# A two-layer hybrid decoder trunk: order pins at the delta rule's inverse and norm, and two kinds of subtraction and addition moved to GpSimd

## The chip, the cores and the metric

The kernel runs on one core of one Trainium2 chip, in one launch. The metric is the device time of that launch in microseconds (us), taken as the median of several runs. The core has a matrix engine (TensorE, PE in the profile, with its weight loads shown as PEld), three engines that work on elements (VectorE or DVE, ScalarE or ACT, GpSimd or POOL) and queues that start data transfers (here those of SyncE, SP). Each engine takes its instructions in the order in which they stand in its own queue; semaphores order the engines among each other.

## The reference

Two layers, 1024 positions, width 1024, all in float32. Each layer normalises its input, projects it once, and gives slices of the projection to three mixers whose gated outputs go through one output projection and are added to the input. Cut to what matters:

```python
h = rmsnorm(x, norm_gain)
proj = h @ w_in
(gq, gk, gv, gb, ga, gz, mq, mkv, mkr, mz, lx, lz) = split(proj)
# A: gated delta rule, 4 heads of 128, chunks of 64 positions
q, k, v = silu(conv4(gq, gk, gv)); q, k = l2norm(q), l2norm(k)
sol = triangular_solve(tril(k*b @ k.T * decay) + I, [v*b, k*b*exp(g)])
state = state * exp(g_last) + k_n.T @ (u_n - w_n @ state)      # over the chunks
o_a = rmsnorm(o, gdn_out_norm) * silu(gz)
# B: attention with low-rank q and k/v, 8 heads, causal softmax
o_b = attention(q, k, v) * silu(mz)
# C: gated linear recurrence (RG-LRU) over 512 channels
u = conv4(lx) + bias; r, i = sigmoid(u @ w_r + b_r), sigmoid(u @ w_i + b_i)
a = exp(-8 r softplus(-L)); h_t = a_t h_(t-1) + sqrt(1 - a_t**2) i_t u_t
o_c = h * silu(lz)
out = x + concat(o_a, o_b, o_c) @ w_out
```

A last rmsnorm follows the second layer.

## The kernel before

A float32 product is made of three matmuls on split operands (high times high, high times low, low times high; `mm3`, whose records in the profile stand on L132, L133 and L134). A high part is a cast (`whi`, `uh`, `oh`), a low part a subtraction (`wlo`, `ul`, `ol`). `split` does the cast on ScalarE and the subtraction on VectorE unless an engine is given.

Each layer has two phases. **Phase A** runs input tiles (`in_tile`), each 128 output channels by 1024 positions: 48 matmuls into an accumulator `pbig`, of which there are two buffers. Its order in the program is that of `phase_a`: for heads 0, 1 (pr=0) and then heads 2, 3 (pr=1) it calls the steps of the delta rule, and between them `go(k)` draws k steps from a generator of *filler* work: input tiles of other mixers, with the convolutions or gates that belong to them. `gdn_pre` builds the chunk matrices, `gdn_inverse` inverts them on VectorE and sends them through DRAM, `gdn_prep` multiplies with the inverse (first matmul on L442, for q = 0 to 3), `gdn_scan` carries the state over the chunks, `gdn_norm` squares the outputs on ScalarE, makes the factor `ms`, scales `at` with it on GpSimd (L105, 16 scalings of 128x128), transposes it on PE (L525, four groups of four) and gates it on VectorE (`gzh`). After pr=1 comes `lru`: for m = 0 to 3 an input tile LX, its convolution `u` (one ScalarE operation, then three VectorE steps over 1023, 1022 and 1021 columns, L99), the split into `uh` and `ul`, the gate matmuls into `pssc`, and later the recurrence; then four tiles LZ that gate it, and the output projection of the delta rule's and the LRU's blocks.

**Phase C** is attention: per head scores (`pS`, L777 to L781), maxima on VectorE (L787 to L792), exponentials on ScalarE, scaling by the reciprocal sum, transposes (L827), and the product with V (L838 to L840). `out_proj_last` is the last block of the output projection: it splits eight weight tiles (`wl`) into high and low parts, adds the result to the residual, and squares and sums the new residual (`add_squares`, L190) for the next norm.

What runs next on an engine is not the program's order. A scheduler (the tile framework's) lists the instructions by dependencies, its own time estimates and a priority that the program can shift: the input tiles' matmuls are put far back (`prio(LOW)`), so that they fill the gaps, and low parts, gates and convolutions far ahead (`prio(-LOW)`). `keep_in_program_order(i)` ties an instruction behind the instruction of the same engine that was written just before it, without a semaphore. The kernel uses it once, in `gate_sums`. Buffers come from rotating pools, so an instruction may also wait for an older reader of its buffer.

Of the kernel before, what the change touches and what calls it, by code (L numbers as in the profile page):

```python
# [63 lines left out]
class Trunk:  # L64
# [357 lines left out]
    def gdn_prep(self, pr, P, q):  # L422

        nc, pa, con = self.nc, self.pa, self.con
        qs = slice(q * H2, (q + 1) * H2)
        M = pa.tile([128, H2], F32, name="mt", tag="am", bufs=2)
        nc.sync.dma_start(M, self.dn[pr][:, qs])
        TT = pa.tile([128, H2], F32, name="tq", tag="tmat", bufs=1)
        nc.sync.dma_start(TT, self.dz[pr][:, qs])
        bv = pa.tile([128, H2], F32, name="bv", tag="bv", bufs=1)  # L430
        bk = pa.tile([128, H2], F32, name="bk", tag="bk", bufs=1)
        kd = [pa.tile([128, H2], F32, name="kd", tag="kd", bufs=4) for _ in range(2)]
        for c, u, hd, cs in self.combos(q):
            j = q * 4 + c
            gj = u * 4 + 2 * pr + hd
            self.gts(bv[:, cs], P["vtok"][q][:, cs], P["br"][:, j : j + 1])
            self.gts(bk[:, cs], P["ktok"][q][:, cs], P["br2e"][:, j : j + 1])
            for par in range(2):
                self.gts(kd[par][:, cs], P["ktok"][q][:, cs], self.dec[:, par, gj : gj + 1])
        pz = self.bank("pr")  # L440
        for c, u, hd, cs in self.combos(q):
            nc.tensor.matmul(pz[:, cs], M[:, cs], TT[:, cs], start=True, stop=True)  # L442
        z = pa.tile([128, H2], F32, name="z", tag="w1", bufs=1)
        q4 = lambda ap: ap.rearrange("p (c j) -> p c j", c=4)
        self.tt(q4(z), q4(pz), con[:, K_MZ : K_MZ + 128].unsqueeze(1).to_broadcast([128, 4, 128]), ALU.mult)
        py = self.bank("pr")
        for c, u, hd, cs in self.combos(q):
            nc.tensor.matmul(py[:, cs], M[:, cs], z[:, cs], start=True, stop=True)
        tf = pa.tile([128, H2], F32, name="tf", tag="w2", bufs=1)
        self.tt(tf, py, TT, ALU.add)  # L450
        pw = self.bank("pr")
        for c, u, hd, cs in self.combos(q):
            nc.tensor.matmul(pw[:, cs], bk[:, cs], tf[:, cs], start=True, stop=True)
        for hd in range(2):

            base = P["wq"][hd][:, 2 * q : 2 * q + 2, 0:64]
            dst = bass.AP(base.tensor, base.offset, [list(base.ap[0]), list(base.ap[1]), [192, 2], [1, 64]])
            nc.scalar.copy(dst, pw.rearrange("p (u h c j) -> p u h c j", u=2, h=2, c=2)[:, :, hd])
        pu = self.bank("pr")
        for c, u, hd, cs in self.combos(q):  # L460
            nc.tensor.matmul(pu[:, cs], tf[:, cs], bv[:, cs], start=True, stop=True)
        uu = pa.tile([128, H2], F32, name="uu", tag="uu", bufs=2)
        nc.scalar.copy(uu, pu)
        P["u"][q], P["kd"][q] = uu, kd
# [41 lines left out]
    def gdn_norm(self, pr, P):  # L506

        nc, pa = self.nc, self.pa
        jk = pa.tile([128, 128], F32, name="junk", tag="junk", bufs=1)
        ms = pa.tile([128, 16], F32, name="ms", tag="ms", bufs=2)  # L510
        for q in range(4):
            for c, u, hd, cs in self.combos(q):
                last = self.act(jk, P["attn"][q][:, cs], AF.Square, accum_out=ms[:, 4 * q + c : 4 * q + c + 1])
        self.tt(ms, ms, P["rq2"], ALU.mult)
        self.behind(self.act(ms, ms, AF.Ln, scale=1.0 / 128.0, bias=self.eps), self.ln_exp_set(last))
        self.act(ms, ms, AF.Exp, scale=-0.5)
        self.tt(ms, ms, P["rq"], ALU.mult)
        for q in range(4):
            o = P["attn"][q]
            for c, u, hd, cs in self.combos(q):  # L520
                self.gts(o[:, cs], o[:, cs], ms[:, 4 * q + c : 4 * q + c + 1])
            pt = self.bank("pr")
            for c, u, hd, cs in self.combos(q):
                j = hd * 256 + (c // 2) * 128
                nc.tensor.transpose(pt[:, j : j + 128], o[:, cs], self.ident)  # L525
            gz = pa.tile([128, H2], F32, name="gzh", tag="gzh", bufs=2)
            for hd in range(2):
                nc.sync.dma_start(gz[:, hd * 256 : hd * 256 + 256], self.gzd[2 * pr + hd][:, q * 256 : q * 256 + 256])
            self.stt(gz, pt, self.onh, gz, ALU.mult, ALU.mult)
            for hd in range(2):  # L530
                nc.sync.dma_start(self.oad[2 * pr + hd][:, q * 256 : q * 256 + 256], gz[:, hd * 256 : hd * 256 + 256])
# [336 lines left out]
    def out_proj_last(self, wsrc, ops, xin, xout, alloc):  # L868

        nc = self.nc  # L870
        W = []
        for m in range(8):
            if m < 4 or m % 2 == 0:
                w = self.pp.tile([128, 2 if m < 4 else 4, 256], F32R, name="wl", tag="P2" if m < 4 else "P4", bufs=4)
            hi, lo = (w[:, j] for j in ((0, 1) if m < 4 else (2 * (m % 2), 2 * (m % 2) + 1)))
            st = self.pw.tile([128, self.wn], F32, name="wst", tag="wst")
            nc.sync.dma_start(st[:, :256], wsrc[m].rearrange("p k c -> p (k c)"))
            with self.prio(-self.LOW):
                self.split(hi, lo, st[:, :256])
            W.append(tuple(a.rearrange("p (k c) -> p k c", k=2) for a in (hi, lo)))  # L880
        for n in range(2):
            xs, accs = [], []
            for m in range(8):
                if m < 6:
                    xt = self.pc.tile([128, H2], F32, name="xk", tag=("q", "qr")[n], bufs=6)
                elif m == 6:
                    both = self.pc.tile([128, 2, H2], F32, name="xk", tag="ob", bufs=6)
                    xt = both[:, 0]
                else:
                    xt = both[:, 1]  # L890
                self.out_tile(*W[m], ops, n, "pj", xt, xin[m], xout and xout[m])
                with self.prio(-self.LOW):
                    if m % 2 == 0 or m == 7:
                        accs.append(None)
                    accs[-1] = self.add_squares(alloc, accs[-1], xt, (nc.vector, nc.gpsimd)[n])
                xs.append(xt)
            yield n, xs, accs

# [77 lines left out]
    def phase_a(self, l):  # L976
# [31 lines left out]
        def fill0():  # L1008
            yield from gz[0]
            yield from itertools.islice(mz, 8 - self.MZ1 - self.MZ2)  # L1010
            P[1] = self.gdn_new()
            yield from qkv(1, P[1])

        def fill1():
            yield from self.lat_kv(l)
            yield from self.lat_q(l)
            yield from gz[1]
            yield from mz

        for pr, fill, n in ((0, fill0(), self.FILL[0]), (1, fill1(), self.FILL[1])):  # L1020
            def go(k):
                for _ in range(k):
                    next(fill, None)
            Q = P[pr]
            self.gdn_tok(pr, Q)
            go(n[0])
            for q in range(4):
                self.gdn_pre(pr, Q, q)
                go(n[1])
            self.gdn_inverse(pr)  # L1030
            go(n[2])
            self.gdn_prep(pr, Q, 0)
            go(n[3])
            for q in range(4):
                if q < 3:
                    self.gdn_prep(pr, Q, q + 1)
                self.gdn_scan(pr, Q, q)
                go(n[4])
            self.gdn_norm(pr, Q)
            go(99)  # L1040

    MZ1 = 4
    MZ2 = 0
# [177 lines left out]
```

## Time and profile before

| | us |
|---|---|
| median of 3 runs | 2149.24 (2148.1 to 2151.57) |
| the profiled execution | 2147.64 |
| its span, first to last instruction | 2145.7 |
| mean granted TensorE clock | 0.992 of full |

The profile is of one execution. A row of its timeline gives the start in us from the span's begin, the duration in us, engine, line, operation, output and inputs, and shape; xN stands for N such instructions in a row, and a bracket gives the idle time of the engine just before and what ended it. Names drop their buffer numbers. Where the seconds go by engine: PE is busy nearly all the time; VectorE 1302.2, ScalarE 858.0 and GpSimd 719.8 us of the span.

### The profile page before, as it was taken

The page shows a single profiled execution, that of the slowest core. Times are in us where ns is not written, and L with a number is a line of the kernel's source. Part 1 is how long each engine was busy: PE and PEld are TensorE (multiplying, and loading weights), DVE is VectorE, ACT ScalarE, POOL GpSimd, SP SyncE. Part 2 cuts the span into 40 slices and gives each one's busy share as a digit, 9 for nine tenths or more (in the row PEclk, how much of TensorE's full clock was granted, in tenths as well). Part 3 has the DMA queues.
Part 4 walks back from the last instruction along what each step waited for, and adds up shares of the span by engine and source line. Part 5 has one row for each costly group of instructions (what it writes and reads, how often), then busy time and mean ns, then how long its engine had stood idle before and what let it go on. Part 6 is the DMA issues. An engine that isn't in the chain of part 4 may idle for free. (4 is left out here: it accounts for less than half of the span.)

```text
span 2145.7 us, 28793 instructions
## 1 busy us (share of the span) xinstructions
PE 2050.1 (96%) x10380; PEld 1681.6 (78%) x10380; DVE 1302.2 (61%) x2506; ACT 858.0 (40%) x1771; POOL 719.8 (34%) x776
## 2 busy tenths in 40 slices
PE   7999999999989999999899999999998999999997
PEld 4888878787777788888678888787776878888875
DVE  6556546545741777776764575474467237676766
ACT  5241243145620554443542313522375125444534
POOL 2132332333541433332342223333336323332322
PEclk9999999999999999999999999999999999999999
DMA  5123113413254015335511321134223520335163
GB/s 176 55 81 116 55 50 104 124 54 104 69 186 134 23 51 176 115 114 179 188 55 40 113 86 50 64 103 133 69 69 108 181 97 24 111 117 173 56 216 123
DMA packets 135102, 222.07 MB, mean 103 GB/s; under 512 B 37808, under 2 KB 60336, under 8 KB 134960
## 3 DMA queue, kind: packets, MB, share of 16 engines
q1 hardware_dynamic: 134960, 220.24, 31.9%
q8 instruction: 82, 1.34, 0.3%
q14 instruction: 60, 0.49, 0.1%
HBM read 147.31 MB, written 72.88 MB: 103 GB/s over the span
## 5 line engine op out<-in xcount | busy, mean ns | idle before, releaser
L123 POOL TENSOR_TENSOR wlo<-wst,whi 128x1024 fp32r<-128x1024 f32 (+3 forms) x196 | 318.9, 1628 | 849.2 <-DVE whi L122 305.4
L132 PE MATMUL pbig<-h,whi 128*128 128x512 f32 x1216 | 483.9, 398 | 6.7 <-ACT h L138 4.9
L134 PE MATMUL pbig<-h,wlo 128*128 128x512 f32 x1216 | 483.0, 397 | 4.5 <-POOL wlo L123 4.5
L133 PE MATMUL pbig<-h,whi 128*128 128x512 f32 x1216 | 482.4, 397 | 0.1
L132 PEld LDWEIGHTS pbig<-h,whi 128*128 128x128 f32 x1216 | 229.6, 189 | 53.0 <-ACT h L138 6.4
L134 PEld LDWEIGHTS pbig<-h,wlo 128*128 128x128 f32 x1216 | 229.9, 189 | 50.4 <-POOL wlo L123 6.2
L133 PEld LDWEIGHTS pbig<-h,whi 128*128 128x128 f32 x1216 | 229.7, 189 | 44.6 <-issue 1.0
L122 DVE CAST whi<-wst 128x1024 fp32r<-128x1024 f32 x92 | 79.8, 867 | 184.0 <-PE pbig L133 134.2
L86 ACT ACTIVATE P<-pS,mx,scq 128x512 f32<-128x512 f32 (+1 forms) x192 | 128.0, 669 | 155.6 <-DVE mx L790 78.9
L105 POOL TENSOR_SCALAR P<-P,mx 128x128 f32<-128x128 f32 (+6 forms) x112 | 80.4, 719 | 209.4 <-DVE mx L798 119.8
L120 ACT CAST whi<-wst 128x256 fp32r<-128x256 f32 (+2 forms) x104 | 46.6, 448 | 199.6 <-DMA wst<-in_w_uk 96.9
L138 ACT CAST pth<-pstp 128x512 fp32r<-128x512 f32 x192 | 90.6, 478 | 79.1 <-PE pstp L827 77.7
L787 DVE TENSOR_REDUCE mx<-pS 128x1 f32<-128x512 f32 (+1 forms) x192 | 106.6, 555 | 18.1 <-PE pS L781 11.6
L139 DVE TENSOR_TENSOR ptl<-pstp,pth 128x512 fp32r<-128x512 f32 x192 | 104.9, 552 | 15.4 <-ACT pth L138 14.9
L827 PE MATMUL pstp<-con,P 128*128 128x128 f32 x576 | 98.6, 276 | 6.2 <-DVE P L802 5.3
L102 DVE TENSOR_TENSOR xt<-pspj,xt 128x512 f32<-128x512 f32 x96 | 66.3, 690 | 52.5 <-PE pspj L134 24.9
L827 PEld LDWEIGHTS pstp<-con,P 128*128 128x128 f32 x576 | 72.5, 142 | 25.5 <-DVE P L802 7.1
L132 PE MATMUL pspj<-lh,whi 128*128 128x512 f32 x208 | 83.9, 404 | 2.1 <-DVE xt L102 1.8
L838 PE MATMUL pspo<-pth,vh 128*128 128x512 f32 x192 | 79.9, 416 | 4.8 <-ACT pth L138 4.7
L86 ACT ACTIVATE z<-pbig 128x1024 f32<-128x1024 f32 x24 | 24.6, 1026 | 146.2 <-PE pbig L134 143.0
L133 PE MATMUL pspj<-ll,whi 128*128 128x512 f32 x208 | 81.8, 393 | 0.0
L134 PE MATMUL pspj<-lh,wlo 128*128 128x512 f32 x208 | 81.4, 392 | 0.0
(271 smaller groups left out, 4588.6 us busy)
## 6 DMA issues: line engine op xcount, KB each, us to landing
wst<-in_w_in SPq DMA_DIRECT2D x76, 512.0 KB, 3.6
x<-xt SPq DMA_DIRECT2D x128, 256.0 KB, 3.3
xt<-x SPq DMA_DIRECT2D x112, 256.0 KB, 3.3
mzd<-z SPq DMA_DIRECT2D x16, 512.0 KB, 4.5
wst<-in_w_o SPq DMA_DIRECT2D x16, 512.0 KB, 3.5
mz<-mzd SPq DMA_DIRECT2D x32, 256.0 KB, 3.2
wst<-in_w_o SPq DMA_DIRECT2D x64, 128.0 KB, 2.1
xk<-x SPq DMA_DIRECT2D x32, 256.0 KB, 4.6
```

Source lines behind the costliest of these rows:

```text
L86: return self.nc.scalar.activation(out, in_, func, **kw)
L105: self.nc.gpsimd.tensor_scalar(out, a, s, 1.0, ALU.mult, ALU.mult)
L122: nc.vector.tensor_copy(hi[:, :n], st[:, :n])
L123: (eng or nc.gpsimd).tensor_tensor(lo[:, :n], st[:, :n], hi[:, :n].bitcast(F32), ALU.subtract)
L132: nc.tensor.matmul(out, ah, bh, start=(start and j == 0), stop=False)
L133: nc.tensor.matmul(out, ah, bl, start=False, stop=False)
L134: nc.tensor.matmul(out, al, bh, start=False, stop=(stop and j == n - 1))
L138: self.nc.scalar.copy(hi, x)
L139: (eng or self.nc.vector).tensor_tensor(lo, x, hi.bitcast(F32), ALU.subtract)
L787: nc.vector.tensor_reduce(mx[:, j : j + 1], S[j], AX.X, ALU.max, negate=True)
L827: nc.tensor.transpose(tp[:, qi * 128 : qi * 128 + 128], P[qi][:, kb * 128 : kb * 128 + 128], self.ident)
L838: nc.tensor.matmul(po[:, w], vh[:, vs], th[:, w], start=(j == 0), stop=False)
```

## The change

Four edits, each in both layers:

1. In `gdn_prep` the first product on the inverse for q = 0 is tied behind the PE instruction written before it.
2. `gdn_norm` becomes a generator that stops after `ms`. `phase_a` runs it to there, then draws the rest of the filler (`go(99)`), then runs its second half. The first transpose of q = 0 is tied in the same way. So the transposes are written behind all the filler that is left, and pinned there.
3. The last call of `go` for pr = 1 draws one step less.
4. In `out_proj_last` the low parts of the weights, and the sums of squares of the first half of the columns, go from VectorE to GpSimd (8 and 3 per layer).

```diff
@@ gdn_prep
-            nc.tensor.matmul(pz[:, cs], M[:, cs], TT[:, cs], start=True, stop=True)
+            first = nc.tensor.matmul(pz[:, cs], M[:, cs], TT[:, cs], start=True, stop=True)
+            if q == 0 and c == 0:
+
+                self.tc.keep_in_program_order(first)
@@ gdn_norm
         self.tt(ms, ms, P["rq"], ALU.mult)
+        yield
         for q in range(4):
...
-                nc.tensor.transpose(pt[:, j : j + 128], o[:, cs], self.ident)
+                t = nc.tensor.transpose(pt[:, j : j + 128], o[:, cs], self.ident)
+                if q == 0 and c == 0:
+                    self.tc.keep_in_program_order(t)
@@ out_proj_last
-                self.split(hi, lo, st[:, :256])
+                self.split(hi, lo, st[:, :256], nc.gpsimd)
...
-                    accs[-1] = self.add_squares(alloc, accs[-1], xt, (nc.vector, nc.gpsimd)[n])
+                    accs[-1] = self.add_squares(alloc, accs[-1], xt, nc.gpsimd)
@@ phase_a
-                go(n[4])
-            self.gdn_norm(pr, Q)
+
+                go(n[4] - (pr == 1 and q == 3))
+            norm = self.gdn_norm(pr, Q)
+            next(norm)
             go(99)
+            for _ in norm:
+                pass
```

Line numbers shift by up to 10: the transposes of L525 stand on L529 after, L790 on L796.

How the order moves, in the rows of each engine's queue (line, operation, output and inputs with buffer numbers, shape, xN for repeats). First place: PE at the end of the norm of heads 0, 1 in layer 0. `pbig_2371` and `pbig_2540` are filler tiles, L525 the norm's transposes. Before:

```order
L133 MATMUL pbig_2540<-h_110,whi_2536 128x512
L134 MATMUL pbig_2540<-h_102,wlo_2537 128x512
L132 MATMUL pbig_2540<-h_103,whi_2536 128x512
L133 MATMUL pbig_2540<-h_111,whi_2536 128x512
L525 MATMUL pspr_2309<-con_69,at_1052 128x128 x4
L525 MATMUL pspr_2324<-con_69,at_1146 128x128 x4
L134 MATMUL pbig_2540<-h_103,wlo_2537 128x512
L132 MATMUL pbig_2540<-h_104,whi_2536 128x512
L133 MATMUL pbig_2540<-h_112,whi_2536 128x512
L525 MATMUL pspr_2339<-con_69,at_1240 128x128 x4
L134 MATMUL pbig_2540<-h_104,wlo_2537 128x512
```

After (L316 are the sums of squares of the filler's q head, `pbig_2815` the next filler tile):

```order
L132 MATMUL pbig_2540<-h_107,whi_2536 128x512
L133 MATMUL pbig_2540<-h_115,whi_2536 128x512
L134 MATMUL pbig_2540<-h_107,wlo_2537 128x512
L316 MATMUL pspr_2370<-ep_70,th_2365 128x1 x8
L529 MATMUL pspr_2384<-con_69,at_1052 128x128 x4
L529 MATMUL pspr_2399<-con_69,at_1146 128x128 x4
L132 MATMUL pbig_2540<-h_108,whi_2536 128x512
L133 MATMUL pbig_2540<-h_116,whi_2536 128x512
L529 MATMUL pspr_2414<-con_69,at_1240 128x128 x4
L134 MATMUL pbig_2540<-h_108,wlo_2537 128x512
L132 MATMUL pbig_2815<-h_101,whi_2811 128x512
L529 MATMUL pspr_2429<-con_69,at_1334 128x128 x4
```

The transposes moved behind 37 more matmuls of `pbig_2540` and the eight L316, and fewer matmuls stand between them.

Second place: behind the norm of heads 2, 3 in layer 0, where the LRU begins. `pbig_3965` is the tile LX of m = 0, `pbig_4061` that of m = 1, `pbig_4157` that of m = 2; `u_4014` and `u_4110` are the convolutions of m = 0 and 1. VectorE before:

```order
L99 SCALAR_TENSOR_TENSOR gzh_3916<-pspr_3911,onh_345,gzh_3916 128x512
L99 SCALAR_TENSOR_TENSOR gzh_3931<-pspr_3926,onh_345,gzh_3931 128x512
L99 SCALAR_TENSOR_TENSOR gzh_3946<-pspr_3941,onh_345,gzh_3946 128x512
L980 TENSOR_SCALAR onh_9705<-par_9301 128x1
L122 CAST whi_4153<-wst_4151 128x1024
L99 SCALAR_TENSOR_TENSOR u_4014<-pbig_3965,par_185,u_4014 128x1023
L99 SCALAR_TENSOR_TENSOR u_4014<-pbig_3965,par_185,u_4014 128x1022
L99 SCALAR_TENSOR_TENSOR u_4014<-pbig_3965,par_185,u_4014 128x1021
L139 TENSOR_TENSOR ul_4020<-u_4014,uh_4019 128x512
L102 TENSOR_TENSOR u_4014<-u_4014,lg_4042 128x1024
L122 CAST whi_4249<-wst_4247 128x1024
L99 SCALAR_TENSOR_TENSOR u_4110<-pbig_4061,par_185,u_4110 128x1023
```

VectorE after:

```order
L99 SCALAR_TENSOR_TENSOR gzh_3901<-pspr_3896,onh_345,gzh_3901 128x512
L99 SCALAR_TENSOR_TENSOR gzh_3916<-pspr_3911,onh_345,gzh_3916 128x512
L99 SCALAR_TENSOR_TENSOR gzh_3931<-pspr_3926,onh_345,gzh_3931 128x512
L99 SCALAR_TENSOR_TENSOR gzh_3946<-pspr_3941,onh_345,gzh_3946 128x512
L986 TENSOR_SCALAR onh_9705<-par_9301 128x1
L122 CAST whi_4249<-wst_4247 128x1024
L99 SCALAR_TENSOR_TENSOR u_4014<-pbig_3965,par_185,u_4014 128x1023
L99 SCALAR_TENSOR_TENSOR u_4110<-pbig_4061,par_185,u_4110 128x1023
L99 SCALAR_TENSOR_TENSOR u_4014<-pbig_3965,par_185,u_4014 128x1022
L99 SCALAR_TENSOR_TENSOR u_4110<-pbig_4061,par_185,u_4110 128x1022
L99 SCALAR_TENSOR_TENSOR u_4014<-pbig_3965,par_185,u_4014 128x1021
L99 SCALAR_TENSOR_TENSOR u_4110<-pbig_4061,par_185,u_4110 128x1021
```

Before, the convolution of m = 0 was through before that of m = 1 began; after, the two alternate. PE at the gate matmuls of m = 0, before:

```order
L134 MATMUL pbig_4061<-h_103,wlo_4058 128x512
L132 MATMUL pbig_4061<-h_104,whi_4057 128x512
L133 MATMUL pbig_4061<-h_112,whi_4057 128x512
L134 MATMUL pbig_4061<-h_104,wlo_4058 128x512
L132 MATMUL pssc_4032<-uh_4019,whi_4027 128x512
L132 MATMUL pbig_4061<-h_105,whi_4057 128x512
L133 MATMUL pbig_4061<-h_113,whi_4057 128x512
L133 MATMUL pssc_4032<-ul_4020,whi_4027 128x512
L134 MATMUL pssc_4032<-uh_4019,wlo_4028 128x512
L132 MATMUL pssc_4037<-uh_4019,whi_4027 128x512
L133 MATMUL pssc_4037<-ul_4020,whi_4027 128x512
L134 MATMUL pssc_4037<-uh_4019,wlo_4028 128x512
```

and after:

```order
L134 MATMUL pbig_4061<-h_107,wlo_4058 128x512
L132 MATMUL pbig_4061<-h_108,whi_4057 128x512
L133 MATMUL pbig_4061<-h_116,whi_4057 128x512
L134 MATMUL pbig_4061<-h_108,wlo_4058 128x512
L132 MATMUL pbig_4157<-h_101,whi_4153 128x512
L132 MATMUL pssc_4032<-uh_4019,whi_4027 128x512
L133 MATMUL pssc_4032<-ul_4020,whi_4027 128x512
L134 MATMUL pssc_4032<-uh_4019,wlo_4028 128x512
L132 MATMUL pssc_4037<-uh_4019,whi_4027 128x512
L133 MATMUL pssc_4037<-ul_4020,whi_4027 128x512
L134 MATMUL pssc_4037<-uh_4019,wlo_4028 128x512
```

The tile of m = 0 now ends ahead of the norm (not shown), and the gate matmuls stand behind the whole tile of m = 1 and one matmul of m = 2, where they stood within the tile of m = 1.

Third place: VectorE at the end of attention in layer 0, where `wl_9319` is the first weight tile and `mx_9060` the maxima of a block of scores. Before:

```order
L99 SCALAR_TENSOR_TENSOR of_9056<-pspo_8800,mz_8798 128x512
L787 TENSOR_REDUCE mx_9060<-pS_9061 128x1
L102 TENSOR_TENSOR pS_9068<-pS_9068,con_69 128x128
L787 TENSOR_REDUCE mx_9060<-pS_9068 128x1
L139 TENSOR_TENSOR wl_9319<-wst_9320,wl_9319 128x256
L790 TENSOR_SCALAR mx_9060<-mx_9060,scq_3244 128x1
L139 TENSOR_TENSOR ptl_9094<-pstp_9088,pth_9093 128x512
L787 TENSOR_REDUCE mx_9097<-pS_9098 128x1
```

After:

```order
L99 SCALAR_TENSOR_TENSOR of_9056<-pspo_8800,mz_8798 128x512
L793 TENSOR_REDUCE mx_9060<-pS_9061 128x1
L102 TENSOR_TENSOR pS_9068<-pS_9068,con_69 128x128
L793 TENSOR_REDUCE mx_9060<-pS_9068 128x1
L796 TENSOR_SCALAR mx_9060<-mx_9060,scq_3244 128x1
L139 TENSOR_TENSOR ptl_9094<-pstp_9088,pth_9093 128x512
L793 TENSOR_REDUCE mx_9097<-pS_9098 128x1
```

The low part of `wl_9319` left VectorE's queue (it stands on GpSimd's behind the low part of attention's output), and the scaling of the maxima moved up by one.

## The prediction

> **What bounds the kernel now.** I read the busy shares first, then the waits of TensorE (PE) over the whole span, then the timeline around those waits that the change touches.
>
> ```profile
> PE 2050.1 (96%) x10380; PEld 1681.6 (78%) x10380; DVE 1302.2 (61%) x2506; ACT 858.0 (40%) x1771; POOL 719.8 (34%) x776
> ...
> PE pspr L132 <- ACT oh L138: 7.7, 2, 3.9
> PE pspr L525 <- POOL at L105: 6.2, 4, 1.7
> PE pssc L133 <- POOL ul L139: 6.2, 7, 1.5
> PE pspo L838 <- ACT pth L138: 4.7, 4, 1.8
> PE pS L777 <- ACT P L86: 4.4, 8, 1.4
> ```
>
> PE is busy 96% of a span of 2145.7 us and issues the same matmuls after the change, in another order, so time is won or lost only where PE stands still. The rows of waits give total us, times, longest us. A wait on `at` (the transposes of the norm) comes four times: two norms per layer, two layers. That is the wait the change aims at. The next rows are the full rate of PE and this wait at the first norm of layer 0.
>
> ```profile
> 293.79 0.39 PE L134 MATMUL pbig<-h,wlo 128*128 128x512 f32 x1
> ...
> 296.28 0.39 PE L133 MATMUL pbig<-h,whi 128*128 128x512 f32 x1
> 298.33 2.76 PE L525 MATMUL pspr<-con,at 128*128 128x128 f32 x8 [1.66 <-POOL at L105]
> ...
> 301.62 0.85 PE L525 MATMUL pspr<-con,at 128*128 128x128 f32 x4
> ...
> 303.70 0.60 PE L525 MATMUL pspr<-con,at 128*128 128x128 f32 x4
> ...
> 295.56 2.37 POOL L123 TENSOR_TENSOR wlo<-wst,whi 128x1024 fp32r<-128x1024 f32 x1 [5.31 <-PE pbig L134]
> 297.91 5.58 POOL L105 TENSOR_SCALAR at<-at,ms 128x128 f32<-128x128 f32 x16
> ```
>
> Eleven products lie between starts 293.79 and 296.28: 0.227 us each, my unit for input products below. The transposes wait 1.66 us for GpSimd's first scaling and then go at its pace of 5.58/16 = 0.35 us: eight take 2.76 us where four unhindered ones take 0.60.
>
> **The change, part by part (per layer).**
>
> *First norm (heads 0, 1).* Before, 22 products stand between the scan's last matmul group and the first transpose; by the order after, 59 products and another 8 small L316 matmuls do. The 37 more are 37 x 0.227 = 8.4 us, and the scalings end 5.15 us after the first transpose started (297.91 + 5.58 = 303.49 against 298.33). So the whole loss goes: 1.66 + (2.76 - 1.20) + (0.85 - 0.60) = **-3.5 us**. What is late next there is `th` for the L316 matmuls, six operations behind the tile that ends at 296.67 (three of them the convolution's steps, 3.92 us by the row of `u` below); 45 products (10.2 us) now cover it. I take -3.5, bounds -3.5 and -1.5.
>
> *Product on the inverse (L442).* For heads 0, 1 it stays on its row. For heads 2, 3 the pin moves the whole scan one input tile (48 products, 10.9 us) later among the products. Its own wait (on the reload of `tq` between q=0 and q=1) keeps the same products between: 0, bounds -1 and +1.
>
> *Second norm (heads 2, 3).* Here the tile pinned ahead of the norm is the LRU's first, LX0, and only 8 products of LX1 (1 in layer 1) follow before the transposes.
>
> ```profile
> 482.79 2.75 PE L525 MATMUL pspr<-con,at 128*128 128x128 f32 x8 [1.60 <-POOL at L105]
> ...
> 480.02 2.37 POOL L123 TENSOR_TENSOR wlo<-wst,whi 128x1024 fp32r<-128x1024 f32 x1 [17.01 <-PE pbig L134]
> 482.36 5.57 POOL L105 TENSOR_SCALAR at<-at,ms 128x128 f32<-128x128 f32 x16
> ...
> 1540.09 1.28 ACT L86 ACT_TABLE_LOAD   x1
> ...
> 1543.53 5.57 POOL L105 TENSOR_SCALAR at<-at,ms 128x128 f32<-128x128 f32 x16 [2.79 <-DVE ms L102]
> 1543.96 2.75 PE L525 MATMUL pspr<-con,at 128*128 128x128 f32 x8 [1.33 <-POOL at L105]
> ```
>
> The end of the scalings sets the end of the transposes. In layer 0 GpSimd's order is unchanged (a `wlo` of 2.37 us still ahead of them), and the products inside the wait fall from 30 to 23: 7 x 0.227 = +1.6. In layer 1 they fall from 37 to 22 (+3.4), while two table loads (1.28 each) and `z` leave ScalarE's path to `ms` and a `wlo` of 2.4 steps in between the scalings: about 1.6 earlier, net +1.8. I take **+1.7**, bounds 0 and +3.
>
> *LRU behind the second norm.* This is the term that decides. Before, the convolution of LX0 (`u`) ran alone on VectorE while PE had the products of LX1:
>
> ```profile
> 496.09 1.21 ACT L86 ACTIVATE u<-pbig,par 128x1024 f32<-128x1024 f32 x1 [14.16 <-PE pbig L134]
> ...
> 497.33 3.92 DVE L99 SCALAR_TENSOR_TENSOR u<-pbig,par,u 128x1023 f32<-128x1023 f32 x3 [0.71 <-ACT u L86]
> ...
> 503.40 1.14 ACT L138 CAST uh<-u 128x512 fp32r<-128x512 f32 x2
> ...
> 504.27 1.27 POOL L139 TENSOR_TENSOR ul<-u,uh 128x512 fp32r<-128x512 f32 x1
> ...
> 505.60 0.50 PE L133 MATMUL pssc<-ul,whi 128*128 128x512 f32 x1 [0.57 <-POOL ul L139]
> ```
>
> In the order after, VectorE alternates the two convolutions: 1023 of LX0, 1023 of LX1, 1022, 1022, 1021, 1021. PE's row is: all of LX1, one product of LX2, then the gate matmuls on `uh` of LX0. Each queue is served in order, so LX0's last step stands behind LX1's first, and that cannot start before PE has finished LX1 and ScalarE has made `u`. PE then waits for a chain that starts at its own last product: ScalarE 1.21, four VectorE steps of 3.92/3 = 1.31 (5.2), the first half of the cast 1.14/2 = 0.57, GpSimd's `ul` 1.27: 8.3 us. LX2's first product is no help: the accumulators rotate over two buffers, and LX0's is released by that same 1021 step. Behind the waiting gate matmuls stand the rest of LX2, LX3 and all LZ tiles. PE fits 3 matmuls in (0.7) and had 0.57 and 0.28 of wait there before, so the new idle is about +7.2.
>
> The clock adds to it. The end of phase A shows what an idle stretch leaves:
>
> ```profile
> 599.72 0.79 PE L132 MATMUL pspr<-oh,whi 128*128 128x512 f32 x1 [3.83 <-ACT oh L138]
> 601.83 0.79 PE L133 MATMUL pspr<-ol,whi 128*128 128x512 f32 x1 [1.32 <-DVE ol L139]
> ...
> 599.00:603.00 4.00, 1.96 (x4) 1.26 (x5) 3.92 (x5) 2.15 (x3) 2.23 (x1) 0.50 0.17 37
> 602.00:606.00 4.00, 4.00 (x11) 3.14 (x12) 2.71 (x4) 0.67 (x2) 0.00 (x0) 0.56 0.85 305
> 606.00:612.00 6.00, 6.00 (x28) 4.97 (x27) 2.52 (x3) 2.05 (x2) 1.52 (x1) 1.00 0.52 165
> ```
>
> In the windows the granted clock stands behind the five engines. After 3.83 + 1.32 us of idle it is 0.50 and 0.56; 4 us hold 11 matmuls instead of 17.6, a loss of 6.6 x 0.227 = 1.5 us. An idle stretch of 7 us will cost 1.5 to 3; I take +2. The Trainium skill, "TensorE: Matmul & The Clock Gate", What's actually happening, has a free-running window of about 3.4 us: half the clock after an idle one, full again after a busy one. By that rule the price would be one to two windows at half rate, an estimated 1.6 to 3.2 us; the rows above agree with the lower end.
>
> Together **+9.2**, bounds +6 (no clock loss, `ul` waits further on shrink) and +12 (the later `ul` of m=3 waits as well).
>
> *Attention's end.* Before, a VectorE low part stood ahead of what the softmax waited for:
>
> ```profile
> 1023.34 1.24 DVE L139 TENSOR_TENSOR wl<-wst,wl 128x256 fp32r<-128x256 f32 x1
> ...
> 1025.99 0.43 DVE L139 TENSOR_TENSOR wl<-wst,wl 128x256 fp32r<-128x256 f32 x1
> ...
> 1023.02 1.28 POOL L139 TENSOR_TENSOR o<-of,o 128x512 fp32r<-128x512 f32 x1 [12.44 <-ACT o L138]
> ...
> 1025.72 0.58 PE L777 MATMUL pS<-k,q 128*128 128x256 f32 x1 [1.44 <-ACT P L86]
> ```
>
> With it gone from VectorE, P's exponential comes about 1 us earlier, of the 1.44 that PE waits. The 16 low parts and 6 square sums run on GpSimd instead: a 128x256 low part takes 0.74 there (the row below), a 128x512 sum about what `o` takes, 1.28. GpSimd was idle 12.44 us before `o`, and the last addend of the sums is ScalarE's anyway, so I take **-1**, bounds -3 (a half-clock stretch goes too) and +1.
>
> ```profile
> 503.57 0.74 POOL L123 TENSOR_TENSOR wlo<-wst,whi 128x256 fp32r<-128x256 f32 x1 [4.40 <-ACT whi L120]
> ```
>
> The 1.24 us of `wl` beside `o`, against 0.43 alone, show that VectorE and GpSimd hinder each other. The Trainium skill, "SBUF — State Buffer", SBUF: two separate sides, says why: the two share a pair of ports under an exclusive lock, which a VectorE operation with two SBUF inputs or in a 2-port mode cannot pass while GpSimd holds it. This case's pair of rows agrees. It speaks against moving work to GpSimd, and is rival 3.
>
> *The dropped filler call* is empty: the second filler has 11 steps and calls for 12. Cost 0.
>
> **Sum.** Per layer -3.5 + 0 + 1.7 + 9.2 - 1 = +6.4; two layers +12.8. On the profiled execution, 2147.64: 2160.4. The median of the runs lies 1.6 above that execution, so 2162.0 in its terms. I forecast **2161.5**.
>
> **The rivals.**
>
> 1. *The new wait is paid back at the end of phase A.* PE waits there 1.33 + 0.68 + 3.83 + 1.32 = 7.2 us for GpSimd, ScalarE and VectorE; if these were merely behind, a later PE would find them done.
>
> ```profile
> 590.26 0.50 PE L134 MATMUL pspr<-oah,wlo 128*128 128x512 f32 x1 [1.33 <-POOL wlo L123]
> 593.05 0.50 PE L133 MATMUL pspr<-oal,whi 128*128 128x512 f32 x1 [0.68 <-POOL oal L139]
> ...
> 587.37 2.83 POOL L123 TENSOR_TENSOR wlo<-wst,whi 128x1024 fp32r<-128x1024 f32 x1
> ...
> 594.99 1.05 ACT L138 CAST lh<-latf 128x1024 fp32r<-128x1024 f32 x1 [3.58 <-DMA latf<-latd]
> ```
>
> Then 6 us of the 9.2 come back: per layer +0.4, time 2148 to 2150, not slower. For it: GpSimd's chain of low parts ends at 593, after the products do, and five table loads fewer stand on ScalarE's queue. Against: the cast `lh` stands ahead of the last gate on ScalarE and waits for a transfer that starts only behind the last input tile, so 3.83 and 1.32 stay. It decides if that transfer can start 4 us earlier relative to PE. Chance 0.14.
>
> 2. *The change does what it says and nothing new waits*: both norms' losses go (3.5 and about 3.4), attention's end -1, per layer -7.9, time 2133. It needs the alternating convolutions to finish without LX1, which the order excludes. Chance 0.06.
>
> 3. *The lock makes attention's end worse.* A GpSimd operation of 0.74 to 1.28 us that holds up a VectorE operation PE waits for, three times per layer, turns -1 into +2: 2168. Chance 0.08.
>
> **How the numbers follow.** Forecast 0.68 (its own range 2155 to 2169), rivals 0.14, 0.06, 0.08, other mishaps 0.04. The range 2150 to 2169 takes in the forecast, rival 3 and rival 1's upper edge. A measurement of this kernel tells 0.2% (4.3 us) from no change. Slower by more: forecast and rival 3, 0.77 with part of the rest; same: most of rival 1 and the forecast's low edge, 0.14; faster: rival 2 and a little of rival 1, 0.09.
>
> **What would show it.** Right: `pspr` L529 has no wait at the first norms; a new wait of 5 to 7 us on `uh` or on `pbig` near 500 us and 1560 us, then a lower granted clock; more time at the second norms. Wrong: no wait over 2 us there, or the waits on `oh` gone at the end of phase A.

## The result and the profile after

The changed kernel takes 2175.13 us (median of 4 runs, 2172.81 to 2176.05) against 2148.67 for the kernel before on the same chip: a ratio of 1.0124, 95% interval 1.0111 to 1.0137. It is slower by 26.5 us, above the top of the predicted range. The profiled execution took 2172.81 us, with a span of 2171.0 and a mean granted clock of 0.983 (0.992 before). Of the 25.3 us by which the span grew, 8.1 are longer busy time of PE for the same 10380 matmuls (2058.2 instead of 2050.1 us) and 17.2 are longer idle time.

The page's busy times and the waits of PE after the change (us in total, times, longest us):

```profile
PE 2058.2 (95%) x10380; PEld 1686.2 (78%) x10380; DVE 1292.8 (60%) x2484; ACT 846.5 (39%) x1761; POOL 736.8 (34%) x798
...
PE pbig L132 <- DVE u L99: 13.9, 4, 6.7
PE pspr L132 <- ACT oh L138: 10.9, 2, 6.0
PE pstp L833 <- DVE P L808: 7.8, 7, 2.4
PE pssc L133 <- POOL ul L139: 6.8, 8, 1.2
PE pS L783 <- ACT P L86: 5.7, 8, 2.4
...
PE pspr L529 <- POOL at L105: 3.4, 3, 1.7
...
PE pbig L132 <- DVE lz L99: 2.9, 2, 1.5
PE pspr L386 <- DVE a L99: 2.8, 2, 1.4
...
PE pspr L338 <- DVE gzh L99: 2.7, 2, 1.4
...
PE pspo L844 <- ACT pth L138: 0.6, 1, 0.6
```

The wait on `at` fell from 6.2 to 3.4 us, that of L838 (now L844) from 4.7 to 0.6. In their place stand 13.9 us on `u`, which were not there at all, 10.9 instead of 7.7 on `oh`, and the small new waits on `lz`, `gzh` and `a`.

Where it went, from starts that both timelines have (us; the lag is after minus before):

| first or last start of | layer 0 before, after | lag | layer 1 before, after | lag |
|---|---|---|---|---|
| product on the inverse, heads 0, 1 | 226.49, 226.10 | -0.4 | 1283.88, 1296.40 | +12.5 |
| token transposes, heads 2, 3 (L338) | 311.88, 316.33 | +4.5 | 1369.77, 1387.01 | +17.2 |
| last transpose of the second norm | 488.72, 498.47 | +9.8 | 1549.15, 1567.38 | +18.2 |
| output projection of phase A | 588.32, 602.22 | +13.9 | 1645.56, 1671.89 | +26.3 |
| attention's scores | 699.64, 716.11 | +16.5 | 1757.38, 1784.69 | +27.3 |
| end | | | 2145.67, 2171.03 | +25.4 |

A lag alone misleads: a point can come later because more products were issued ahead of it, and these are done. So I take 0.227 us off the lag for each product that the changed kernel is ahead. At L338 the changed kernel has issued 33 products more (7.5 us at 0.227), so the first norm won 4.5 + 0.4 - 7.5 = -2.6 us and -2.8 in layer 1. At the second norm's last transpose it is 43 products ahead in layer 0 (9.8 us) and 29 in layer 1 (6.6), and from there to the output projection it loses them all and more: 13.9 - 9.8 + 9.8 = 13.9 us, and 26.3 - 18.2 + 6.6 = 14.7. That stretch is the LRU. The output projection adds 2.6 and 1.0; attention gives back 4.0 and 2.0 in this one execution.

The start of the LRU in layer 0 after the change, from the timeline and from the windows (in these, after the five engines, the granted clock):

```profile
490.29 1.19 ACT L86 ACTIVATE u<-pbig,par 128x1024 f32<-128x1024 f32 x1
...
506.90 0.69 DVE L122 CAST whi<-wst 128x1024 fp32r<-128x1024 f32 x1 [2.47 <-PE pbig L133]
507.51 7.22 DVE L99 SCALAR_TENSOR_TENSOR u<-pbig,par,u 128x1023 f32<-128x1023 f32 x6
...
507.06 1.20 ACT L86 ACTIVATE u<-pbig,par 128x1024 f32<-128x1024 f32 x1 [15.57 <-PE pbig L134]
...
513.69 0.76 PE L132 MATMUL pbig<-h,whi 128*128 128x512 f32 x1 [6.67 <-DVE u L99]
...
515.65 0.80 PE L133 MATMUL pssc<-ul,whi 128*128 128x512 f32 x1 [0.55 <-POOL ul L139]
...
500.00:507.00 7.00, 7.00 (x31) 5.44 (x29) 1.76 (x4) 0.00 (x0) 0.00 (x0) 1.00 0.47 146
507.00:514.00 7.00, 0.33 (x2) 0.29 (x1) 7.00 (x7) 1.86 (x3) 3.04 (x2) 0.76 0.52 172
514.00:518.00 4.00, 3.45 (x8) 2.15 (x8) 2.07 (x2) 2.74 (x4) 1.27 (x1) 0.50 0.17 65
518.00:521.00 3.00, 3.00 (x9) 2.37 (x8) 0.00 (x0) 0.69 (x1) 0.00 (x0) 0.53 0.00 0
```

The predicted wait is there: PE has nothing to do between 507 and 513.7 while VectorE works through six convolution steps in a row, and it then runs at half clock. But the rows show a second reason that I had missed: in front of all six stands a cast of weights, and that one waited for PE too, for the last product that uses the older weights in its buffer. So even the first convolution, whose step on ScalarE had been done since 491.5, could not start before PE ran dry.

The other new wait lies at the first norm. In the kernel before, the gate loads (SyncE's row) go out while VectorE still has the convolution `y` of the last filler head and what follows it, and the token transposes of heads 2, 3 do not wait:

```profile
302.25 1.27 DVE L99 SCALAR_TENSOR_TENSOR y<-pbig,par,y 128x1021 f32<-128x1021 f32 x1
...
307.13 1.40 DVE L99 SCALAR_TENSOR_TENSOR gzh<-pspr,onh,gzh 128x512 f32<-128x512 f32 x2
...
303.26 2.25 SPq L528 DMA_DIRECT2D gzh<-gzd  x4
...
311.88 0.60 PE L338 MATMUL pspr<-con,kT 128*128 128x128 f32 x4
```

After the change (with SyncE's queue of transfers in the last two rows):

```profile
308.18 0.60 PE L529 MATMUL pspr<-con,at 128*128 128x128 f32 x4
...
316.33 0.66 PE L338 MATMUL pspr<-con,kT 128*128 128x128 f32 x4 [1.39 <-DVE gzh L99]
...
306.36 1.41 DVE L99 SCALAR_TENSOR_TENSOR gzh<-pspr,onh,gzh 128x512 f32<-128x512 f32 x2 [3.63 <-PE pspr L529]
...
315.52 1.41 DVE L99 SCALAR_TENSOR_TENSOR gzh<-pspr,onh,gzh 128x512 f32<-128x512 f32 x2 [7.15 <-DMA gzh<-gzd]
...
310.93 0.33 SPq L115 DMA_DIRECT2D wst<-in_w_in  x1
311.36 1.81 SPq L534 DMA_DIRECT2D gzh<-gzd  x4
```

The gate of the norm has two buffers. The third and fourth gate load (311.36) wait until the first two results are stored, and stand behind a weight load in SyncE's queue. Until they land, two accumulators stay occupied, and the token transposes of heads 2, 3 need them. Which of the two holds the loads longer, the stores or the weight load, was not separated. Before, the norm's transposes and these loads ran beside the last filler head's convolution; after, they come behind it, and the second pair behind them.

### The profile page after: what moved, and what is told of

It is laid out like the page before. It is cut to its first block, busy times and chain, and to the rows that moved or that the text cites. A ratio compares the mean times of both kernels' runs of the same rounds, so it can differ in the third digit from the quotient of the medians.

```text
span 2171.0 us, 28793 instructions
## 1 busy us (share of the span) xinstructions
PE 2058.2 (95%) x10380; PEld 1686.2 (78%) x10380; DVE 1292.8 (60%) x2484; ACT 846.5 (39%) x1761; POOL 736.8 (34%) x798
## 5 line engine op out<-in xcount | busy, mean ns | idle before, releaser
L132 PE MATMUL pbig<-h,whi 128*128 128x512 f32 x1216 | 486.5, 400 | 21.4 <-DVE u L99 13.9
L133 PE MATMUL pbig<-h,whi 128*128 128x512 f32 x1216 | 483.5, 398 | 2.2 <-DVE h L139 2.2
L122 DVE CAST whi<-wst 128x1024 fp32r<-128x1024 f32 x92 | 73.9, 803 | 159.9 <-PE pbig L133 100.0
L833 PEld LDWEIGHTS pstp<-con,P 128*128 128x128 f32 x576 | 72.3, 141 | 27.7 <-DVE P L808 10.2
L844 PE MATMUL pspo<-pth,vh 128*128 128x512 f32 x192 | 79.6, 415 | 1.0 <-ACT pth L138 0.6
```

Source lines behind the costliest of these rows:

```text
L122: nc.vector.tensor_copy(hi[:, :n], st[:, :n])
L132: nc.tensor.matmul(out, ah, bh, start=(start and j == 0), stop=False)
L133: nc.tensor.matmul(out, ah, bl, start=False, stop=False)
L833: nc.tensor.transpose(tp[:, qi * 128 : qi * 128 + 128], P[qi][:, kb * 128 : kb * 128 + 128], self.ident)
L844: nc.tensor.matmul(po[:, w], vh[:, vs], th[:, w], start=(j == 0), stop=False)
```

## The experiments

Each ratio is to the kernel before on the same chip, with its 95% interval. The first question was which part of the change moves the queues.

**Pins alone.** All ties of the change, but the norm's second half is written where it was (an excerpt, with comments added):

```diff
+            if q == 0 and c == 0:
+                self.tc.keep_in_program_order(first)      # gdn_prep
...
+                if q == 0 and c == 0:
+                    self.tc.keep_in_program_order(t)      # gdn_norm
...
+            for _ in norm:
+                pass
             go(99)
```

> All pins of the change (the product on the inverse, both norms' first transposes) and the norm cut in two, but its second half is written where it stood before, and attention is untouched. Theory A (the loss comes from writing the first norm's second half behind the last filler head): the queues are those of before, so 2148.7 us, within 0.2%. Theory B (the prediction's: the pins shift the second scan by a tile and so bring the LRU's first tile ahead of the second norm): 2160 us or more.

Measured: 1.0004 (0.9992 to 1.0015), no difference, as theory A says. Every engine's queue holds the same instructions in the same order as before. So the ties do nothing here, and the prediction's sentence that the pin on the inverse moves the second scan by a tile is refuted.

**The first norm's second half written late, nothing else** (an excerpt).

```diff
-            self.gdn_norm(pr, Q)
+            norm = self.gdn_norm(pr, Q)
+            next(norm)
+            if pr == 0:
+                go(99)
+            for _ in norm:
+                pass
             go(99)
```

> Only the first norm's second half is written behind the rest of the filler, with no pin anywhere; the second norm and attention as before. Theory A: the whole loss of the change and its gain at attention's end left out, that is 2148.7 + 31 = 2180 us (16.5 and 14.8 us lost per layer up to the first score matmul of attention in the two traces). Theory B: no more than the first norm's own gain, 2142 us. Theory C (GpSimd's added operations block VectorE): less loss than the change, below 2170 us.

Measured: 2182.37 us, 1.0140 (1.0118 to 1.0162). This alone, without a pin and without a change in attention, brings the whole loss (its interval overlaps with that of the change). Its queues in phase A are those of the changed kernel. Theories B and C fall.

**Attention's part alone** (low parts and square sums on GpSimd).

```diff
-                self.split(hi, lo, st[:, :256])
+                self.split(hi, lo, st[:, :256], nc.gpsimd)
...
-                    accs[-1] = self.add_squares(alloc, accs[-1], xt, (nc.vector, nc.gpsimd)[n])
+                    accs[-1] = self.add_squares(alloc, accs[-1], xt, nc.gpsimd)
```

> Only the weights' low parts and the squares' sums go to GpSimd. From the two traces, between attention's first score matmul and the end of the layer, the change wins 4.0 and 1.9 us: theories A and B 2148.7 - 6 = 2143 us. Theory C: 2150 us or more.

Measured: 0.9994 (0.9980 to 1.0007): no difference that can be measured. The 6 us that two single executions seemed to show lie outside the interval, and so does a loss of more than 1.5 us. The waits of PE in its profile, and in that of the kernel before the two that are not shown above:

```profile
PE pstp L827 <- DVE P L802: 7.9, 7, 2.4
PE pS L777 <- ACT P L86: 7.4, 8, 3.2
PE pspo L840 <- DVE ptl L139: 5.0, 9, 0.9
...
PE pspo L838 <- ACT pth L138: 1.7, 3, 0.8
```

```profile
PE pspo L840 <- DVE ptl L139: 6.1, 10, 2.1
PE pstp L827 <- DVE P L802: 5.3, 6, 0.9
```

L838's wait fell from 4.7 to 1.7 and L840's from 6.1 to 5.0, while L777's grew from 4.4 to 7.4 and L827's from 5.3 to 7.9: 20.5 us together before, 22.0 after. In these two executions other waits took the place of those removed.

**Four gate buffers in the changed kernel.** The third and fourth gate tile take a tag with two buffers that nobody uses at that time:

```diff
-            gz = pa.tile([128, H2], F32, name="gzh", tag="gzh", bufs=2)
+            gz = pa.tile([128, H2], F32, name="gzh", tag=("gzh", "uu")[q // 2], bufs=2)
```

> The changed kernel, with four buffers instead of two for the gate that multiplies the norm's transposes (two groups use another tag that is free then), so that the third and fourth gate load do not wait for the first two to be stored. Theory A, refined: the loss arises because the second pair's token transposes now queue behind transposes whose accumulators wait for these loads; without that wait the second pair starts 24 products earlier, the LRU's convolutions no longer alternate, and the change wins: 2148.7 - 2 x 3.5 (first norm) - 6 (attention) = 2136 us. If the late writing itself is the cause, or the alternation has another one: 2165 us or more.

Measured: 2142.56 us, 0.9966 (0.9952 to 0.9981). One line turns a loss of 26 us into a gain of about 7, which is less than the expected 2136 us: that had counted on 6 us from attention. Its timeline at the first norm and at the LRU's first convolution:

```profile
305.53 1.41 DVE L99 SCALAR_TENSOR_TENSOR gzh<-pspr,onh,gzh 128x512 f32<-128x512 f32 x2 [3.62 <-PE pspr L529]
...
307.45 1.40 DVE L99 SCALAR_TENSOR_TENSOR gzh<-pspr,onh,gzh 128x512 f32<-128x512 f32 x2
...
308.50 0.60 PE L338 MATMUL pspr<-con,kT 128*128 128x128 f32 x4
...
492.04 3.92 DVE L99 SCALAR_TENSOR_TENSOR u<-pbig,par,u 128x1023 f32<-128x1023 f32 x3 [0.72 <-ACT u L86]
```

The wait of 7.15 us for the gate is gone. The token transposes start 7.8 us earlier than in the changed kernel, with 24 products fewer ahead of them (5.4 us at 0.227), and the convolution runs in one piece again. The tile of cover comes back with it: in layer 0, the trace has 1991 matmuls of PE ahead of the first product on the inverse of heads 2, 3 in the kernel before, 2042 in the changed kernel and 1993 here, and a tile has 48.

**The LRU's convolutions kept apart**, in the changed kernel. A tie on VectorE puts the first step of one behind the last step of the other; no other queue changes:

```diff
+            if bias is not None and d == 1 and self.last_conv is not None:
+                self.behind(i, self.last_conv)
```

> The changed kernel with one tie more: on VectorE the first step of an LRU convolution stands behind the last step of the one before, so that the two no longer alternate; the other queues keep their order. Theory A: the wait of 6.7 us on u goes, but on ScalarE the cast uh of m=0 still stands behind u of m=1, which waits for the whole tile of m=1: a wait of 1.2 + 0.4 + 0.6 us and 1.3 for ul stays, 3 us of the 7.2, and part of the half clock goes: 2175 - 2 x 4.2 - 0 to 3 = 2163.5 to 2166.5 us. Rival: the alternation is only where a missing tile of cover shows, and the time is lost further on: 2171 us or more.

Measured: 2171.18 us, 1.0101 (1.0084 to 1.0118): about 5 us better than the change, with intervals that still overlap, and less than the 8.5 to 11.5 us that theory A expected. Its timeline:

```profile
505.29 0.69 DVE L122 CAST whi<-wst 128x1024 fp32r<-128x1024 f32 x1 [3.07 <-PE pbig L133]
505.90 5.10 DVE L99 SCALAR_TENSOR_TENSOR u<-pbig,par,u 128x1023 f32<-128x1023 f32 x4
...
509.96 0.47 PE L132 MATMUL pbig<-h,whi 128*128 128x512 f32 x1 [4.54 <-DVE u L99]
```

The cast that waits for PE still stands in front, and PE still waits 4.54 us for `u` (6.67 in the change). The alternation is worth two of the six steps, not the wait. The time is the one that the rival of this run gave.

**Four gate buffers in the kernel before**, with the line of the fourth run and nothing else.

> The kernel before with four buffers for the norm's gate instead of two, nothing else. If the buffers help by themselves (the gate loads no longer come late): 2142 us, as with the change. If they help only because the transposes are written late: 2148.7 us within 0.2%.

Measured: 1.0011 (0.9997 to 1.0024). The buffers alone bring nothing; they help only where the transposes are written late.

**The late first norm with four buffers, attention as before.**

> First norm's second half written late and four gate buffers, no pins, attention as before. If attention's moves bring nothing: as the change with four buffers, 2142.5 us. If they bring the 4 to 6 us that the traces seemed to show: 2147 us.

Measured: 2141.74 us, 0.9968 (0.9955 to 0.9980), the same as the fourth run within the intervals. It is the plainest version that beats both kernels.

**The queues at the LRU's start untied**, in the changed kernel: besides the tie of the fifth run, that cast stands behind the first convolution, and ScalarE's `u` of m+1 behind the casts `uh` of m (an excerpt).

```diff
+                if self.convs is not None and len(self.convs) == 3:
+                    self.behind(i, self.convs[0])          # load_w's cast
...
+            if self.last_cast is not None:
+                self.behind(i, self.last_cast)             # conv's ScalarE step
```

> The changed kernel, with the LRU's first convolution freed from all that waits for the second input tile: VectorE's steps apart, the cast of the weights for m=3 (which waits for the weights of m=1 to be used up) behind the first convolution, and ScalarE's u of m+1 behind the casts uh of m. The first norm is still written late and the LRU still begins one tile nearer to the second norm. Theory A (the first wait of 7.2 us and its half clock are these queues' doing): 2175 - 2 x (7.2 + 2) = 2157 us, less if the later waits of the stretch go as well. Rival (the cover of one tile is lost and PE waits elsewhere): as the convolutions apart, 2168 us or more.

Measured: 2161.82 us, 1.0063 (1.0046 to 1.0080). About half of the loss is gone, less than theory A's 18 us and more than the rival's. The wait of 6.67 us on `u` is gone: the longest one left on `u` is 1.1 us. The timeline (the lines of the three matmuls and of the split shift by two) shows what came instead:

```profile
506.57 0.40 ACT L120 CAST whi<-wst 128x256 fp32r<-128x256 f32 x1 [16.63 <-DMA wst<-in_w_lru]
...
507.05 0.99 POOL L125 TENSOR_TENSOR wlo<-wst,whi 128x256 fp32r<-128x256 f32 x1 [10.20 <-DMA xt<-in_x]
...
508.00 2.35 POOL L125 TENSOR_TENSOR wlo<-wst,whi 128x1024 fp32r<-128x1024 f32 x1
510.32 1.71 POOL L141 TENSOR_TENSOR ul<-u,uh 128x512 fp32r<-128x512 f32 x1
...
512.08 0.79 PE L135 MATMUL pssc<-ul,whi 128*128 128x512 f32 x1 [3.21 <-POOL ul L141]
```

Now the gate weights come late, and GpSimd makes their low part (0.99 us) only after they land. Behind it stands the low part of an input tile's weights (2.35 us), which belongs to the cast that the tie had moved, and only then comes `ul`. So a part of this wait of 3.21 us is made by the ties of this run. In SyncE's queue the load of the gate weights stands right behind the stores of the norm's results (it is issued at 504.02). Whether they hold it was not tried.

**Four buffers at one norm only**, in the changed kernel, first at the first norm (the line below), then at the second (`pr == 1` in its place):

```diff
+            gz = pa.tile([128, H2], F32, name="gzh", tag=("gzh", "uu")[q // 2 if pr == 0 else 0], bufs=2)
```

> The changed kernel with four gate buffers at the first norm only. Theory A (the second pair's start waits for the first norm's gate loads, and all else follows from that): nearly all of what four buffers at both norms gave, 2142 to 2147 us. Rival D (what costs is the second norm's gate loads and stores, which hold the LRU's weights and convolutions in SyncE's and VectorE's queues): 2165 us or more.

Measured: 2142.63 us, 0.9970 (0.9957 to 0.9984), as theory A says. Rival D falls.

> The changed kernel with four gate buffers at the second norm only. Theory A: the second scan still runs one tile nearer to the LRU, so only the queues at the LRU's start are relieved, as in the run with the queues untied: 2158 to 2166 us. Rival D: 2142 to 2147 us.

Measured: 2163.07 us, 1.0062 (1.0043 to 1.0082). The gate loads of the first norm are the cause: relieving them there restores everything that four buffers at both norms gave. Relieving the second norm leaves about half of the loss, as the untied queues did. Its timeline at the LRU's start:

```profile
499.84 2.59 DVE L99 SCALAR_TENSOR_TENSOR u<-pbig,par,u 128x1023 f32<-128x1023 f32 x2
507.01 0.69 DVE L122 CAST whi<-wst 128x1024 fp32r<-128x1024 f32 x1 [4.57 <-PE pbig L133]
...
509.04 0.47 PE L132 MATMUL pbig<-h,whi 128*128 128x512 f32 x1 [1.90 <-DVE u L99]
```

Two steps of the first convolution now run ahead of the cast that waits for PE, and the wait on `u` falls from 6.67 to 1.90 us, though the scan of heads 2, 3 is as late as in the change (2042 matmuls ahead of it).

## Why the prediction was right and where it was not

The direction was right, and so were the place and the kind of the wait that decides. The size was half of what came, and two things about that wait were wrong: what brings the tile of cover out of place, and what stands ahead of the convolutions. By the prediction's own steps, per layer:

| step | predicted us | in the two profiles, layer 0 and 1 |
|---|---|---|
| first norm | -3.5 | -2.6, -2.8 |
| pin on the inverse | 0 | 0 (first run); from L338 to the scan's last matmul +2.5, +0.3 |
| second norm (from there to its last transpose) | +1.7 | +0.5, +1.6 |
| LRU behind the second norm | +9.2 | +13.9, +14.7 |
| end of phase A (rival 1: pays back up to 6) | 0 | +2.6, +1.0 |
| attention's end | -1 | -4.0, -2.0; timed alone -0.06% in all |

**First norm.** The waits on `at` there vanished as worked out. Of the gain, 1.39 us went to the wait on `gzh` at L338. The prediction named `th` as what is late next and not the gate loads, although the trace of before has VectorE idle 4.16 us for such a load at the second norm.

**The LRU term is the step that failed, in its size:** +9.2 predicted, +13.9 and +14.7 measured, above its bound of +12. Its first wait was right: priced at 7.2 us of new idle, it measured 6.67 + 0.55 in layer 0, where 0.57 had stood before.

The half clock was priced at 2 us and cost 3.5 in layer 0 and 2.4 in layer 1.

```profile
520.89 0.39 PE L132 MATMUL pssc<-uh,whi 128*128 128x512 f32 x1
...
605.71 0.39 PE L133 MATMUL pspr<-oal,whi 128*128 128x512 f32 x1
```

From the restart at 513.69 to the first row, after the change, PE started 14 products in 7.20 us; without the 0.55 us of idle that is 6.65, where 14 x 0.227 = 3.2 would do. The price came out too low because the prediction read it off the window from 602 to 606, which begins 2.3 us after the restart at 599.72. Counted from that restart to the second row, in the trace of before, 10 products took 4.67 us, the idle 1.32 not counted, where 2.27 would do: 2.4 us and not 1.5.

The later waits, which the term put only into its upper bound, add up to 5.7 us in layer 0 (1.20 on `ul` of m=1, 2.78 on `uh` and `ul` of m=2 and 3, 1.47 on `lz`, 0.27 on `u` for an accumulator) against 2.9 before:

```profile
591.21 0.50 PE L132 MATMUL pbig<-h,whi 128*128 128x512 f32 x1 [1.47 <-DVE lz L99]
...
614.98 0.79 PE L132 MATMUL pspr<-oh,whi 128*128 128x512 f32 x1 [5.96 <-ACT oh L138]
```

With 6.7 for the first wait, 3.5 for the clock and 2.8 for the later ones, 12.9 of the 13.9 us of layer 0 are named; the last 1.0 was not broken down. The stretch had lost one tile of cover for good, and I priced only the first place where it lacked.

**The cause in front of it was named wrongly.** The prediction put the shift by one tile down to the pins. The runs show that the ties leave the order as it is (1.0004), and that the place in the program where the first norm's transposes are written does it (1.0140), through the gate loads that then stand before the second pair (0.9970 with four buffers there). The prediction also laid the wait on `u` to the alternation of the convolutions alone; with them apart 4.54 of the 6.67 us stay, behind the cast that waits for PE. In the change itself the cast adds little, as the convolution's first step behind it (from 507.51) runs beside ScalarE's step (507.06 to 508.26); that is why the price of the first wait came out right without it.

**Rivals.** Rival 1 (paid back at the end of phase A) is refuted by the two traces: the wait on `oh` grew from 3.83 to 5.96 us. Rival 2 (both norms' losses go, nothing new waits) did not come; with four gate buffers a gain of about 7 us does, where it had said 16. Rival 3 (the lock at attention's end makes it worse) is not borne out: its +2 us per layer would be 1.0019, and the moves alone measure 0.9994 (0.9980 to 1.0007). The forecast's -1 per layer, 0.9991, lies within that interval: it is neither shown nor refuted.

## What to carry to other kernels

When an instruction is written later so that other work fills its wait, look at what was written behind it: the next chain inherits its place, its accumulators and its loads. A shift of a few microseconds at the head of a long chain comes out at the far end as a missing tile of cover, at several places, so price the whole stretch and not its first wait, and count what a slow clock costs from the restart on. And before tying an order, see whether the queues differ at all: the ties of this change did nothing, and one line of buffering made the late transposes pay.

## What the runs showed of the hardware

The clock took more than I expected from such a change. In the granted clock of the profile, stretches at 0.5 last 3.4, 6.8 or 10.2 us, except for the one that the end of the execution cuts off; the kernel before has 37 us of them in all, the changed kernel 75. After the idle of 6.67 us the stretch ran from 510.6 for 10.2 us, 7 us past the restart of PE. The Trainium skill, "TensorE: Matmul & The Clock Gate", What's actually happening, speaks of a window of about 3.4 us; the lengths agree with multiples of it, and the number of windows is what I had no way to tell.

Some of these stretches change from one execution to the next. The run with the pins alone has the queues of the kernel before, and yet its trace has stretches at 15.8, 483.5 and 1292.4 us where that of before has none, and lacks those at 1025.4 and 1107.3 us. This explains most of the 4.0 us that attention seemed to give back: from layer 0's scores to the first product on the inverse in layer 1, the trace of before has three stretches of 3.4 us (from 1025.4, 1045.9 and 1107.3) and that of the change one (from 1060.1), and 6.8 us less at half the clock are worth an estimated 3.4 us at most. A difference of that size between two single executions said nothing.
